# Sums of quarters on VectorE, other places for the modulation steps, and another order from the scheduler

## The chip, the cores and the metric

The kernel runs on one core of a Trainium2 chip. The metric is the time of one execution on the device, in microseconds (us), the median of several runs. One profiled execution gives the trace from which the rows below are read. All tensors are float32; no product is left at lower precision than two halves give (below).

## What is computed

Two transformer blocks in a chain, on 512 tokens `x` and 256 context tokens `ctx` of 1024 features (768 together). The first has two layers, an even one (gated linear attention and differential attention) and an odd one (a state space mixer), each followed by a gated feed-forward network; the second block is a feed-forward network, a mixer of window attention and a gated scan, and another feed-forward network. What the change touches is the feed-forward network and the modulation vectors:

```python
def swiglu(h, w_in, w_out):            # h: tokens x 1024, w_in: 1024 x 5632, w_out: 2816 x 1024
    gate, up = jnp.split(h @ w_in, 2, axis=-1)
    return (jax.nn.silu(gate) * up) @ w_out

mod_x = jax.nn.silu(c) @ mod_w[layer] + mod_b[layer]        # 6 vectors of 1024 for x,
mod_c = jax.nn.silu(c_ctx) @ mod_w[layer] + mod_b[layer]    # and 6 for the context
...
x = layer_norm(ALPHA * x + gf_x * swiglu(x * (1.0 + scf_x) + shf_x, ...), ...)
...
mod = (jax.nn.silu(c) @ w_ada[l] + b_ada[l])                # second block: 9 vectors of 1024
```

## The kernel before

Every float32 operand of a product is split into a high and a low half (`split`: ScalarE casts the high half, L64, VectorE subtracts to get the low one, L65), and each product is three matmuls. A weight (`weight`, `wcols`, `wrows`) is loaded by a DMA on SyncE's queue and split, all under a priority that lets the scheduler start it early (`WPRIO`, 400). In the trace `whi` and `wlo` are a weight's halves, `hhi` and `hlo` those of the tokens.

The work runs stage by stage: the even mixer to 470 us of the trace, its output projection and layer norm to 543, the first feed-forward network to some 1060, the odd mixer to 1700, the second network to 2098, the third to 2700, the mixer of the second block to 3250, the last network to the end. The first and the third network work on all 768 tokens, and their first product is done by quarters: tokens, weights and results are cut in two by two, and seven products of quarters, with sums before and after, take the place of eight. These two first products run from 543 to 905 and from 2098 to 2475 us.

`Quarters` keeps the tokens. `put` writes a token tile to DRAM and splits it; `sums` (L418) reads the tiles back when all are there and makes three sums `ts` of quarters (L428, L430 on VectorE, L429 on GpSimd), splits them to `tq`, and makes a fourth, `ts4` (L431, GpSimd), which `fourth` later splits in place of a quarter of the tokens. `first_product_quarters` opens with the first two of the 22 column blocks of the weight done plainly (`whole`: L524 is the silu of the gate on ScalarE, L525 the product with the second half on VectorE, both in `lg`), for the first half of the tokens and then for the second. This covers the time until the sums are there. The body then runs through the remaining 20 blocks in pairs of products (`order`). For each block, `load` fetches two weights `sr` and makes two sums on GpSimd (`sx` and one in place), and `weight` makes two more (all four by L502). `run` takes the results apart (`c`, `p`, `u`, `g`, L567 to L586).

The modulation vectors of later stages are made a step at a time in between. `mod_steps` gives ten steps for a set of one or two vectors: eight parts (a 512 KB DMA, and on VectorE L228 or L230, 128x1024, for each vector into its `acc`), `finish` (L236 adds the bias row, matmuls sum over the partitions, a DMA writes the row to DRAM) and `turn` (a DMA reads the row back as `fmrow`, L255, TensorE transposes it, L257). Steps wait in the list `c.fill`, and `run_fill(n)` puts the next n of them into the program: after each block of a product, and at other places.

The order of the instructions on each engine is set by the scheduler of the library, which takes the program in the order in which it is written, with the priorities above (modulation parts have -150), and estimates when each can start.

Of the kernel before, what the change touches and what calls it, by code (L numbers as in the profile page):

```python
# [8 lines left out]
F32 = mybir.dt.float32  # L9
# [3 lines left out]
ALU = mybir.AluOpType  # L13
# [3 lines left out]
P = 128  # L17
D = 1024
KT = D // P
WPRIO = 400  # L20
# [369 lines left out]
class Quarters:  # L390
# [27 lines left out]
    def sums(self, pool):  # L418

        c, nc = self.c, self.c.nc  # L420
        rest = []
        for i in range(self.half):
            f1, f2 = (pool.tile([P, KT, P], F32, tag=f"f{j}", name=c.nm("f"), bufs=2) for j in range(2))
            nc.sync.dma_start(f1, self.fd[i])
            nc.sync.dma_start(f2, self.fd[i + self.half])
            s = pool.tile([P, 3, 4, P], F32, tag="ts", name=c.nm("ts"), bufs=1)
            s4 = pool.tile([P, 4, P], F32, tag="ts4", name=c.nm("ts4"), bufs=self.half)
            nc.vector.tensor_tensor(s[:, 0], f2[:, :4], f1[:, :4], ALU.subtract)  # L428
            nc.gpsimd.tensor_tensor(out=s[:, 2], in0=f2[:, 4:], in1=f2[:, :4], op=ALU.subtract)  # L429
            nc.vector.tensor_tensor(s[:, 1], f2[:, 4:], s[:, 0], ALU.subtract)  # L430
# [44 lines left out]
LEAD = 2  # L475


def first_product_quarters(c, h, T, w_in, gd, nfill, pool):
# [3 lines left out]
    nc = c.nc  # L482
# [16 lines left out]
    raw = {}  # L499

    def sums(o, x, y, op):
        nc.gpsimd.tensor_tensor(out=o, in0=x, in1=y, op=op)  # L502

    def load(j):
        with c.tc.high_priority(offset=WPRIO):
            r = []
# [4 lines left out]
            r.append(pool.tile([P, 4, P], F32, tag="sx", name=c.nm("sx"), bufs=2))  # L511
            raw[j] = r
            sums(r[4], r[0], r[2], ALU.subtract)
            sums(r[2], r[2], r[3], ALU.add)

    with c.tc.tile_pool(name=c.nm("fs"), bufs=1) as fp:
        ws = [[c.wcols(w_in, o + j * P) for o in (0, FFN_H)] for j in range(LEAD)]

        def whole(j, v, outs):
# [7 lines left out]
            c.run_fill(nfill)  # L527
# [3 lines left out]
        fourth = h.sums(fp)  # L531
# [4 lines left out]
        fourth()  # L536
# [7 lines left out]
    with c.tc.tile_pool(name=c.nm("fm"), bufs=1) as mp:  # L544
        W, S, X = {}, {}, {}

        def weight(j, i, hi, lo):
# [5 lines left out]
            if i == 1:  # L553
                sums(r[0], r[3], r[4], ALU.subtract)
            elif i == 2:
                sums(r[1], r[1], r[0], ALU.subtract)
            W[j, i] = hi, lo

        def run(j, i):
# [23 lines left out]
            elif i == 3:  # L583
# [592 lines left out]
def main(c, I, out, stop=None):  # L1176
# [7 lines left out]

    def accs(pool):
        return lambda: pool.tile([P, D], F32, tag="acc", name=c.nm("acc"))
# [91 lines left out]
    with tc.tile_pool(name="mix0", bufs=1) as mp:  # L1278
        mix = mp.tile([P, 6, D], F32, name="mix")
        og, od = mix[:, :, :512], mix[:, :, 512:]  # L1280
        with tc.tile_pool(name="dif", bufs=1) as dp:
# [10 lines left out]
            with tc.tile_pool(name="gla", bufs=1) as gp:  # L1292
# [5 lines left out]
                c.fill += block1(0, 2, "gm0", "row") + block1(0, 4, "scf0", "fm") + block1(0, 3, "shf0", "fm")  # L1298
# [55 lines left out]
    with tc.tile_pool(name="modp1", bufs=2) as mq:  # L1354
        modp[0] = accs(mq)
        c.fill += block1(0, 5, "gf0", "row") + block1(1, 1, "scm1", "fm") + block1(1, 0, "shm1", "fm")
        c.fill += block1(1, 2, "gm1", "row", False) + block1(1, 4, "scf1", "fm", False)
        c.fill += block1(1, 3, "shf1", "fm", False)
# [3 lines left out]
        ffn(c, h, 768, I["ffn_w_in"][0], I["ffn_w_out"][0], ln, (1, 1))  # L1362
# [32 lines left out]
    with tc.tile_pool(name="modp2", bufs=2) as mq:  # L1395
        modp[0] = accs(mq)
        c.fill += block1(1, 5, "gf1", "row", False) + block2(0, "fm") + block2(1, "fm") + block2(2, "row")
# [19 lines left out]
    with tc.tile_pool(name="modp3", bufs=2) as mq:  # L1417
        modp[0] = accs(mq)
        c.fill += block2(3, "fm") + block2(4, "fm") + block2(5, "row", False) + block2(6, "fm", False)
        c.fill += block2(7, "fm", False) + block2(8, "row", False)  # L1420
# [3 lines left out]
        ffn(c, h, 768, I["ffn1_w_in_2"][0], I["ffn1_w_out_2"][0], ad, (1, 1))  # L1424
# [745 lines left out]
```

## Time and profile before

| | us |
|---|---|
| median of 3 runs | 3641.51 (3630.83 to 3643.37) |
| the profiled run | 3632.67 |
| its span, first to last instruction | 3630.9 |
| TensorE busy (PE) | 3412.6 |
| VectorE busy (DVE) | 2372.8 |
| ScalarE busy (ACT) | 1641.7 |
| GpSimd busy (POOL) | 649.9 |

The span is 1.8 us shorter than the profiled run, and that run is 8.8 us faster than the median. The mean granted clock of TensorE over the span is 0.974 of full speed; most of the loss lies in a few stretches.

### The profile page before, as it was taken

The page shows a single profiled execution, that of the slowest core. Times are in us where ns is not written, and L with a number is a line of the kernel's source. Part 1 is how long each engine was busy: PE and PEld are TensorE (multiplying, and loading weights), DVE is VectorE, ACT ScalarE, POOL GpSimd, SP SyncE. Part 2 cuts the span into 40 slices and gives each one's busy share as a digit, 9 for nine tenths or more (in the row PEclk, how much of TensorE's full clock was granted, in tenths as well). Part 3 has the DMA queues.
Part 4 walks back from the last instruction along what each step waited for, and adds up shares of the span by engine and source line. Part 5 has one row for each costly group of instructions (what it writes and reads, how often), then busy time and mean ns, then how long its engine had stood idle before and what let it go on. Part 6 is the DMA issues. An engine that isn't in the chain of part 4 may idle for free.

```text
span 3630.9 us, 48754 instructions
## 1 busy us (share of the span) xinstructions
PE 3412.6 (94%) x18316; PEld 2903.6 (80%) x18316; DVE 2372.8 (65%) x3578; ACT 1641.7 (45%) x2719; POOL 649.9 (18%) x481
## 2 busy tenths in 40 slices
PE   8999987999989999988999979999999999999998
PEld 5877776999778877767887769998787798878887
DVE  6766667676687577766566786766766585663235
ACT  5335533444345555533334634343556454553234
POOL 0001124433020354443000133430000000000000
PEclk9999998999999999989999989999999999999999
DMA  6330135443774333344666753436751122354356
GB/s 226 111 88 27 47 116 181 134 125 102 244 249 149 87 101 103 101 157 160 219 196 203 261 189 104 134 114 221 252 183 40 52 63 73 108 180 151 119 169 217
DMA packets 446834, 522.53 MB, mean 144 GB/s; under 512 B 21272, under 2 KB 357268, under 8 KB 446597
## 3 DMA queue, kind: packets, MB, share of 16 engines
q1 hardware_dynamic: 446597, 519.41, 45.0%
q8 instruction: 144, 2.36, 0.3%
q14 instruction: 93, 0.76, 0.1%
HBM read 452.49 MB, written 62.64 MB: 142 GB/s over the span
## 4 chain that ended last, share of the span: by engine, by line
PE 34%; issue 9%; DVE 4%; DMA 4%; ACT 2%; POOL 1%; SPq 0%; DVEq 0%; POOLq 0%; ACTq 0%
PE big L99 7%; PE big L113 5%; PE px L113 5%; PE px L496 4%; PE px L99 4%; PE big L496 3%; DMA gr<-gd 1%; DVE wlo L65 1%; PE mm L1606 1%; PE mm L1779 1%; PE big L1571 1%; ACT whi L64 1%; PE mm L1600 1%; PE big L1569 0%; DVE acc L230 0%
## 5 line engine op out<-in xcount | busy, mean ns | idle before, releaser
L65 DVE TENSOR_TENSOR wlo<-raw,whi 128x1024 fp32r<-128x1024 f32 (+1 forms) x444 | 542.3, 1226 | 476.3 <-ACT whi L64 440.9
L64 ACT CAST whi<-raw 128x1024 fp32r<-128x1024 f32 (+1 forms) x444 | 457.7, 1033 | 673.7 <-PE big L99 216.4
L99 PE MATMUL big<-hhi,whi 128*128 128x512 f32 (+1 forms) x1312 | 444.9, 364 | 10.0 <-ACT hhi L64 5.8
L99 PE MATMUL big<-hlo,whi 128*128 128x512 f32 (+1 forms) x1312 | 437.6, 359 | 5.3 <-DVE hlo L65 5.3
L99 PE MATMUL big<-hhi,wlo 128*128 128x512 f32 (+1 forms) x1312 | 439.4, 360 | 0.0
L133 POOL TENSOR_TENSOR s<-s,mhalf 128x1 f32<-128x1 f32 (+1 forms) x106 | 76.3, 721 | 1989.0 <-DVE s L131 1976.0
L99 PEld LDWEIGHTS big<-hhi,whi 128*128 128x128 f32 x1312 | 237.6, 192 | 55.1 <-issue 7.8
L99 PEld LDWEIGHTS big<-hlo,whi 128*128 128x128 f32 x1312 | 236.4, 191 | 42.9 <-DVE hlo L65 6.6
L99 PEld LDWEIGHTS big<-hhi,wlo 128*128 128x128 f32 x1312 | 236.3, 191 | 37.2 <-issue 1.9
L230 DVE SCALAR_TENSOR_TENSOR acc<-graw,silu_c,acc 128x1024 f32<-128x1024 f32 x168 | 223.9, 1355 | 33.5 <-DMA graw<-in_mod_w_dram 16.4
L65 DVE TENSOR_TENSOR wlo<-sr,whi 128x512 fp32r<-128x512 f32 x240 | 187.0, 813 | 60.6 <-ACT whi L64 59.9
L64 ACT CAST whi<-sr 128x512 fp32r<-128x512 f32 x240 | 139.3, 618 | 183.5 <-PE big L496 84.4
L113 PE MATMUL px<-whi,hhi 128*128 128x256 f32 (+1 forms) x712 | 213.2, 302 | 0.1
L113 PE MATMUL px<-wlo,hhi 128*128 128x256 f32 (+1 forms) x712 | 211.1, 299 | 0.0
L113 PE MATMUL px<-whi,hlo 128*128 128x256 f32 (+1 forms) x712 | 210.5, 299 | 0.0
L113 PE MATMUL big<-wlo,ghi 128*128 128x512 f32 x616 | 193.5, 395 | 2.4 <-DVE wlo L65 2.3
L113 PE MATMUL big<-whi,glo 128*128 128x512 f32 x616 | 192.3, 393 | 0.0
L113 PE MATMUL big<-whi,ghi 128*128 128x512 f32 x616 | 192.2, 394 | 0.0
L496 PE MATMUL px<-tq,whi 128*128 128x384 f32 x640 | 165.1, 338 | 4.8 <-DVE tq L65 2.5
L496 PE MATMUL big<-hhi,whi 128*128 128x384 f32 x416 | 143.6, 345 | 26.2 <-DVE lg L525 22.9
L64 ACT CAST ghi<-gr 128x256 fp32r<-128x256 f32 (+1 forms) x176 | 79.7, 458 | 150.0 <-DMA gr<-gd 91.6
L496 PE MATMUL big<-hhi,wlo 128*128 128x384 f32 x416 | 142.8, 344 | 1.7 <-DVE wlo L65 1.7
(594 smaller groups left out, 8265.0 us busy)
## 6 DMA issues: line engine op xcount, KB each, us to landing
raw<-in_ffn_w_out_dram SPq DMA_DIRECT2D x176, 512.0 KB
raw<-in_ffn_w_in_dram SPq DMA_DIRECT2D x96, 512.0 KB
graw<-in_mod_w_dram SPq DMA_DIRECT2D x80, 512.0 KB
sr<-in_ffn_w_in_dram SPq DMA_DIRECT2D x80, 512.0 KB
graw<-in_w_ada_dram SPq DMA_DIRECT2D x72, 512.0 KB
raw<-in_mix_w_in_dram SPq DMA_DIRECT2D x42, 512.0 KB
raw<-in_ssd_w_in_dram SPq DMA_DIRECT2D x41, 512.0 KB
gr<-gd SPq DMA_DIRECT2D x88, 192.0 KB
```

What stands on the lines that cost most here:

```text
L64: self.nc.scalar.copy(hi, src)
L65: self.nc.vector.tensor_tensor(lo, src, hi.bitcast(F32), ALU.subtract)
L99: self.nc.tensor.matmul(out, lhsT=w_[:, k, :], rhs=x_[:, k, t0 : t0 + tn], start=st, stop=sp)
L113: self.nc.tensor.matmul(out, lhsT=h_[:, t0 : t0 + P], rhs=w_[:, n0 : n0 + nn], start=st, stop=sp)
L133: nc.gpsimd.tensor_tensor(out=r, in0=v, in1=self.mhalf[:, :n], op=ALU.pow)
L230: nc.vector.scalar_tensor_tensor(a, raw, v[:, k : k + 1], a, ALU.mult, ALU.add)
L496: nc.tensor.matmul(out, lhsT=w_[:, k], rhs=b_[:, k], start=start and k == 0 and w_ is wh and b_ is bh, stop=stop and k == 3 and w_ is wl, ...
L1571: nc.tensor.matmul(sc[:, o : o + kn], lhsT=qs[b][r, tt], rhs=kl[kv][r, k0 : k0 + kn], start=False, stop=True)
L1600: nc.tensor.transpose(pt[:, i - i0 : i - i0 + P], p[:, i : i + P], c.ident)
L1606: nc.tensor.matmul(po[r, :], lhsT=v[:, u, kv * 64 : kv * 64 + 64], rhs=pT[:, i * P : (i + 1) * P], start=i == 0, stop=i == len(keys) - 1)
L1779: nc.tensor.matmul(pa[:, ts_], lhsT=QK[:, 1, ts_], rhs=Q[:, ts_], start=True, stop=True)
```

## The change

Five things are changed.

- The sums of quarters go from GpSimd to VectorE: the two of each token tile in `Quarters.sums` and the four of each block in `first_product_quarters`. The first two of a block are made where its weight is split first and no longer in `load`; `ts4` is made after the split and kept in another pool, and `fourth` runs after four pairs of the body instead of ahead of it.
- No modulation steps are put in by `whole`, nor by the first two blocks of the body. The rest takes two at each block instead of one.
- The first pairs of weights of the body have a priority of 50 in place of 400.
- `mods` sets the order of the modulation steps: the last step of a set (`turn`) comes behind the fifth step of the next.
- The scheduler orders the whole program by its timeline model.

```diff
     def sums(self, pool, keep):
...
-            s4 = pool.tile([P, 4, P], F32, tag="ts4", name=c.nm("ts4"), bufs=self.half)
+            s4 = keep.tile([P, 4, P], F32, tag="ts4", name=c.nm("ts4"), bufs=self.half)
             nc.vector.tensor_tensor(s[:, 0], f2[:, :4], f1[:, :4], ALU.subtract)
-            nc.gpsimd.tensor_tensor(out=s[:, 2], in0=f2[:, 4:], in1=f2[:, :4], op=ALU.subtract)
             nc.vector.tensor_tensor(s[:, 1], f2[:, 4:], s[:, 0], ALU.subtract)
-            nc.gpsimd.tensor_tensor(out=s4, in0=f1[:, 4:], in1=s[:, 1], op=ALU.subtract)
+            nc.vector.tensor_tensor(s[:, 2], f2[:, 4:], f2[:, :4], ALU.subtract)
             o = slice(i * P, (i + 1) * P)
             c.split(s, self.t[0][:, :, :, o], self.t[1][:, :, :, o])
+            nc.vector.tensor_tensor(s4, f1[:, 4:], s[:, 1], ALU.subtract)
...
     def sums(o, x, y, op):
-        nc.gpsimd.tensor_tensor(out=o, in0=x, in1=y, op=op)
+        nc.vector.tensor_tensor(o, x, y, op)
...
-            sums(r[4], r[0], r[2], ALU.subtract)
-            sums(r[2], r[2], r[3], ALU.add)
...
-            c.run_fill(nfill)
...
-        fourth()
...
             if i == 1:
+                sums(r[4], r[0], r[2], ALU.subtract)
+                sums(r[2], r[2], r[3], ALU.add)
                 sums(r[0], r[3], r[4], ALU.subtract)
...
-                c.run_fill(nfill)
+                if j >= LEAD + 2:
+                    c.run_fill(nfill)
...
-            with c.tc.high_priority(offset=WPRIO):
+            if s == 4:
+                fourth()
+            with c.tc.high_priority(offset=WPRIO if s > 8 else 50):
...
+    def mods(*sets):
+
+        late = None
+        for steps in sets:
+            for i, f in enumerate(steps[:-1]):
+                c.fill.append(f)
+                if i == 4 and late:
+                    c.fill.append(late)
+            late = steps[-1]
+        c.fill.append(late)
...
-        ffn(c, h, 768, I["ffn_w_in"][0], I["ffn_w_out"][0], ln, (1, 1))
+        ffn(c, h, 768, I["ffn_w_in"][0], I["ffn_w_out"][0], ln)
...
-    with _tile.TileContext(nc) as tc:
+    with _tile.TileContext(nc, schedule_with_timeline_sim=True) as tc:
```

What the scheduler makes of it is seen in the order of the instructions. First VectorE where the first product by quarters begins, from the first `lg` (gate times second half of a plain block) to the second. `acc` is a modulation vector, `ts` a sum of token quarters, `sr` a raw weight. Before:

```order
L525 TENSOR_TENSOR lg_5256<-big_5179,lg_5256 128x384
L230 SCALAR_TENSOR_TENSOR acc_5260<-graw_5426,silu_c,acc_5260 128x1024
L230 SCALAR_TENSOR_TENSOR acc_5261<-graw_5426,silu_c,acc_5261 128x1024
L230 SCALAR_TENSOR_TENSOR acc_5260<-graw_5482,silu_c,acc_5260 128x1024
L65 TENSOR_TENSOR wlo_5497<-sr_5358,whi_5496 128x512 x2
L230 SCALAR_TENSOR_TENSOR acc_5261<-graw_5482,silu_c,acc_5261 128x1024
L65 TENSOR_TENSOR wlo_5535<-sr_5365,whi_5534 128x512 x2
L65 TENSOR_TENSOR wlo_5573<-sr_5358,whi_5572 128x512
L65 TENSOR_TENSOR wlo_5573<-sr_5360,whi_5572 128x512
L525 TENSOR_TENSOR lg_5314<-big_5180,lg_5314 128x384
```

And now:

```order
L523 TENSOR_TENSOR lg_5256<-big_5179,lg_5256 128x384
L228 TENSOR_SCALAR acc_5951<-graw_5953,silu_c 128x1024
L228 TENSOR_SCALAR acc_5952<-graw_5953,silu_c 128x1024
L230 SCALAR_TENSOR_TENSOR acc_5951<-graw_5957,silu_c,acc_5951 128x1024
L230 SCALAR_TENSOR_TENSOR acc_5952<-graw_5957,silu_c,acc_5952 128x1024
L230 SCALAR_TENSOR_TENSOR acc_5951<-graw_6083,silu_c,acc_5951 128x1024
L428 TENSOR_TENSOR ts_5316<-f_5313,f_5312 128x512
L430 TENSOR_TENSOR ts_5316<-f_5313 128x512
L230 SCALAR_TENSOR_TENSOR acc_5952<-graw_6083,silu_c,acc_5952 128x1024
L523 TENSOR_TENSOR lg_5308<-big_5180,lg_5308 128x384
```

The splits of the body's first weights no longer stand ahead of the second `lg`; four steps of the modulation became six, and eleven more follow before the third `tq` (three in the order before).

Next VectorE at the start of the second product by quarters, up to the `hlo` with which the last token tile is split. `hTf` is that tile, turned; L982 and L131 are its norm. Before:

```order
L65 TENSOR_TENSOR hlo_17292<-hTf_18089,hhi_17291 128x8x128
L131 TENSOR_SCALAR s_18132<-s_18130 128x1
L230 SCALAR_TENSOR_TENSOR acc_18280<-graw_18501,silu_c,acc_18280 128x1024
L230 SCALAR_TENSOR_TENSOR acc_18279<-graw_18722,silu_c,acc_18279 128x1024
L230 SCALAR_TENSOR_TENSOR acc_18280<-graw_18722,silu_c,acc_18280 128x1024
L230 SCALAR_TENSOR_TENSOR acc_18279<-graw_18848,silu_c,acc_18279 128x1024
L282 TENSOR_SCALAR hTf_18137<-mm_18138,ada_0x,fm_m0x 128x128
L282 TENSOR_SCALAR hTf_18137<-mm_18147,ada_0x,fm_m0x 128x128
L230 SCALAR_TENSOR_TENSOR acc_18280<-graw_18848,silu_c,acc_18280 128x1024
L65 TENSOR_TENSOR hlo_17292<-hTf_18137,hhi_17291 128x8x128
```

And now, for both of the last two tiles:

```order
L236 TENSOR_TENSOR acc_18971<-acc_18971,brow_19536 1x1024
L983 TENSOR_SCALAR s_18124<-s_18118,s_18122 128x1
L1081 TENSOR_TENSOR y_15032<-y_15032,lng_17283 128x1024
L282 TENSOR_SCALAR hTf_18089<-mm_18090,ada_0x,fm_m0x 128x128
L1085 TENSOR_TENSOR y_15032<-y_15032,lnb_17285 128x1024
L282 TENSOR_SCALAR hTf_18089<-mm_18099,ada_0x,fm_m0x 128x128
L131 TENSOR_SCALAR s_18132<-s_18130 128x1
L65 TENSOR_TENSOR hlo_17292<-hTf_18089,hhi_17291 128x8x128
L282 TENSOR_SCALAR hTf_18137<-mm_18138,ada_0x,fm_m0x 128x128
L282 TENSOR_SCALAR hTf_18137<-mm_18147,ada_0x,fm_m0x 128x128
L65 TENSOR_TENSOR hlo_17292<-hTf_18137,hhi_17291 128x8x128
```

The steps between the two `hlo` are gone; all 18 of that set, its last (L236) at the top of this piece, now stand ahead of both.

Last TensorE at the end of the first attention. L918 and L919 are its scores, L950 its transposes, L959 its values; L113 are matmuls of a projection that fills its gaps. Before:

```order
L918 MATMUL big_4203<-dks_3737,dqs_3735 128x512
L919 MATMUL big_4203<-dks_3738,dqs_3735 128x512
L959 MATMUL mm_4181<-ddv,mix 128x128 x2
L918 MATMUL big_4203<-dks_3737,dqs_3735 128x256
L919 MATMUL big_4203<-dks_3738,dqs_3735 128x256
L113 MATMUL px_3916<-wlo_3803,hhi_379 128x256
L113 MATMUL px_3916<-whi_3802,hlo_380 128x256
L113 MATMUL px_3916<-whi_3808,hhi_379 128x256
```

And now, 70 rows earlier, with no projection left:

```order
L951 MATMUL mm_3583<-cfs,dp_3526 128x128 x4
L919 MATMUL big_3760<-dks_3317,dqs_3315 128x512
L920 MATMUL big_3760<-dks_3318,dqs_3315 128x512
L919 MATMUL big_3760<-dks_3317,dqs_3315 128x256
L920 MATMUL big_3760<-dks_3318,dqs_3315 128x256
L951 MATMUL mm_3589<-cfs,dp_3526 128x128 x2
L960 MATMUL mm_3593<-ddv,mix 128x128 x2
L951 MATMUL mm_3774<-cfs,dp_3566 128x128 x4
```

The last matmul of the projection stood 26 rows ahead of the attention's end and now stands 107 rows ahead of it.

## Rows read from the trace of the kernel before

**Rows 1.** The page, part 1: busy us, share of the span, instructions of each engine.

```profile
PE 3412.6 (94%) x18316; PEld 2903.6 (80%) x18316; DVE 2372.8 (65%) x3578; ACT 1641.7 (45%) x2719; POOL 649.9 (18%) x481
```

**Rows 2.** Stretches: length, busy PE, PEld, DVE, ACT, POOL, granted clock, DMA share, GB/s.

```profile
440.00:460.00 20.00, 15.42 (x83) 12.13 (x82) 12.14 (x33) 12.91 (x34) 2.57 (x4) 0.83 0.18 54
580.00:630.00 50.00, 30.40 (x124) 28.33 (x123) 38.30 (x37) 16.99 (x28) 25.87 (x17) 0.73 0.52 174
630.00:905.00 275.00, 266.80 (x1514) 261.72 (x1513) 195.77 (x258) 118.08 (x227) 108.01 (x69) 0.99 0.38 120
2110.00:2180.00 70.00, 44.68 (x216) 42.69 (x215) 57.74 (x62) 29.33 (x52) 24.85 (x16) 0.76 0.53 172
2180.00:2475.00 295.00, 284.74 (x1607) 279.25 (x1606) 196.75 (x258) 123.86 (x237) 107.41 (x72) 0.99 0.35 111
2700.00:3100.00 400.00, 396.42 (x2513) 334.08 (x2512) 262.46 (x598) 214.78 (x382) 6.45 (x5) 1.00 0.22 64
```

**Rows 3.** TensorE in time, 580 to 630: start, duration, instruction, [idle before <- releaser].

```profile
591.67 0.69 PE L496 MATMUL big<-hhi,whi 128*128 128x384 f32 x1 [5.52 <-DVE lg L525]
...
610.92 0.69 PE L496 MATMUL big<-hhi,whi 128*128 128x384 f32 x1 [5.80 <-DVE lg L525]
...
620.95 0.69 PE L496 MATMUL px<-tq,whi 128*128 128x384 f32 x1 [2.51 <-DVE tq L65]
```

**Rows 4.** The same of TensorE, 2110 to 2180.

```profile
2118.78 1.97 PE L275 MATMUL mm<-cfs,xr 128*128 128x128 f32 x8 [5.21 <-ACT xr L1172]
...
2134.50 1.01 PE L496 MATMUL px<-hhi,whi 128*128 128x384 f32 x2 [2.96 <-ACT hhi L64]
...
2170.44 0.69 PE L496 MATMUL big<-hhi,whi 128*128 128x384 f32 x1 [11.53 <-DVE lg L525]
```

**Rows 5.** ScalarE in time at both starts.

```profile
587.62 1.14 ACT L64 CAST whi<-sr 128x512 fp32r<-128x512 f32 x2 [6.54 <-POOL sr L502]
...
2154.56 1.14 ACT L64 CAST whi<-sr 128x512 fp32r<-128x512 f32 x2 [6.95 <-POOL sr L502]
```

**Rows 6.** VectorE in time at both starts.

```profile
575.21 3.67 DVE L230 SCALAR_TENSOR_TENSOR acc<-graw,silu_c,acc 128x1024 f32<-128x1024 f32 x3
...
610.32 0.55 DVE L525 TENSOR_TENSOR lg<-big,lg 128x384 f32<-128x384 f32 x1
...
619.15 1.75 DVE L65 TENSOR_TENSOR tq<-ts,tq 128x1536 fp32r<-128x1536 f32 x1
...
2143.50 0.68 DVE L428 TENSOR_TENSOR ts<-f,f 128x512 f32<-128x512 f32 x1
...
2158.08 1.76 DVE L428 TENSOR_TENSOR ts<-f,f 128x512 f32<-128x512 f32 x1
...
2175.16 2.49 DVE L65 TENSOR_TENSOR wlo<-sr,whi 128x512 fp32r<-128x512 f32 x4
```

**Rows 7.** Groups of instructions: count, busy us, mean ns, idle before and releaser.

```profile
L502 POOL TENSOR_TENSOR sr<-sr 128x512 f32<-128x512 f32 x80 | 121.6, 1520 | 88.1 <-DVE wlo L65 84.0
L431 POOL TENSOR_TENSOR ts<-f,ts 128x512 f32<-128x512 f32 x6 | 10.5, 1757 | 6.7 <-DVE ts L430 6.7
...
L230 DVE SCALAR_TENSOR_TENSOR acc<-graw,silu_c,acc 128x1024 f32<-128x1024 f32 x168 | 223.9, 1355 | 33.5 <-DMA graw<-in_mod_w_dram 16.4 <-DMA graw<-in_w_ada_dram 16.3
L65 DVE TENSOR_TENSOR wlo<-sr,whi 128x512 fp32r<-128x512 f32 x240 | 187.0, 813 | 60.6 <-ACT whi L64 59.9 <-PE px L496 0.3
```

**Rows 8.** TensorE's waits for a turned row (us, times, longest), and one row's DMAs.

```profile
PE mm L257 <- DMA fmrow<-row_m4c: 4.0, 1, 4.0
PE mm L257 <- DMA fmrow<-row_m6x: 2.6, 1, 2.6
PE mm L257 <- DMA fmrow<-row_m7x: 2.0, 1, 2.0
...
L248 SPq DMA_DIRECT2D row_m0c<-acc x1: 235/235/235, 1854.7 to 1854.7; - x1
L255 SPq DMA_DIRECT2D fmrow<-row_m0c x1: 264/264/264, 1860.8 to 1860.8; - x1
```

More of the change, by code (lines that the diff above doesn't have):

```diff
@@ L416, in factors, with sums @@
                 {(0, 0): q(0), (1, 0): q(1), (0, 1): q(2), (1, 1): q(3)})
-    def sums(self, pool):
+    def sums(self, pool, keep):
         c, nc = self.c, self.c.nc
@@ L501, in sums @@
     def sums(o, x, y, op):
-        nc.gpsimd.tensor_tensor(out=o, in0=x, in1=y, op=op)
+        nc.vector.tensor_tensor(o, x, y, op)
     def load(j):
+        r = []
         with c.tc.high_priority(offset=WPRIO):
-            r = []
             for b, o in enumerate((0, FFN_H)):
@@ L510, in load @@
                 r += [x[:, :4], x[:, 4:]]
-            r.append(pool.tile([P, 4, P], F32, tag="sx", name=c.nm("sx"), bufs=2))
-            raw[j] = r
-            sums(r[4], r[0], r[2], ALU.subtract)
-            sums(r[2], r[2], r[3], ALU.add)
+        r.append(pool.tile([P, 4, P], F32, tag="sx", name=c.nm("sx"), bufs=2))
+        raw[j] = r
     with c.tc.tile_pool(name=c.nm("fs"), bufs=1) as fp:
@@ L526, in whole @@
             nc.sync.dma_start(gd[j][:, v * n : v * n + n], g)
-            c.run_fill(nfill)
         for j in range(LEAD):
             whole(j, 0, (one(j), two(j)))
-        fourth = h.sums(fp)
+        fourth = h.sums(fp, pool)
         for j in range(LEAD, LEAD + 2):
@@ L1297, in main @@
                 modp[0] = lambda: df.pair()[:, :D]
-                c.fill += block1(0, 2, "gm0", "row") + block1(0, 4, "scf0", "fm") + block1(0, 3, "shf0", "fm")
+                mods(block1(0, 2, "gm0", "row"), block1(0, 4, "scf0", "fm"), block1(0, 3, "shf0", "fm"))
                 c.run_fill(3)
@@ L1355, in main @@
         modp[0] = accs(mq)
-        c.fill += block1(0, 5, "gf0", "row") + block1(1, 1, "scm1", "fm") + block1(1, 0, "shm1", "fm")
-        c.fill += block1(1, 2, "gm1", "row", False) + block1(1, 4, "scf1", "fm", False)
-        c.fill += block1(1, 3, "shf1", "fm", False)
+        mods(block1(0, 5, "gf0", "row"), block1(1, 1, "scm1", "fm"), block1(1, 0, "shm1", "fm"),
+             block1(1, 2, "gm1", "row", False), block1(1, 4, "scf1", "fm", False), block1(1, 3, "shf1", "fm", False))
         ln = LnTail(c, None, I, 0, 1, 6, {v: f"gf0{v}" for v in "xc"}, xdt(0),
@@ L1396, in main @@
         modp[0] = accs(mq)
-        c.fill += block1(1, 5, "gf1", "row", False) + block2(0, "fm") + block2(1, "fm") + block2(2, "row")
+        mods(block1(1, 5, "gf1", "row", False), block2(0, "fm"), block2(1, "fm"), block2(2, "row"))
         ln = LnTail(c, None, I, 1, 1, 4, {"x": "gf1x"}, xdt(2), lambda: ada_sc(0, 0, "xc"), xd[3], "x", 768,
@@ L1418, in main @@
         modp[0] = accs(mq)
-        c.fill += block2(3, "fm") + block2(4, "fm") + block2(5, "row", False) + block2(6, "fm", False)
-        c.fill += block2(7, "fm", False) + block2(8, "row", False)
+        mods(block2(3, "fm"), block2(4, "fm"), block2(5, "row", False), block2(6, "fm", False),
+             block2(7, "fm", False), block2(8, "row", False))
         ad = AdaTail(c, None, 6, lambda pool: ada_gate(pool, 0, 2, 0.5, "xc"),
@@ L1423, in main @@
                      out if stop == "f1" else None)
-        ffn(c, h, 768, I["ffn1_w_in_2"][0], I["ffn1_w_out_2"][0], ad, (1, 1))
+        ffn(c, h, 768, I["ffn1_w_in_2"][0], I["ffn1_w_out_2"][0], ad)
         h = ad.h
```

## The prediction, made before the changed kernel was run

> **What bounds the kernel now.** I read first the page's table of busy times, then the stretches, then the waits of TensorE in the stretches where it is not full. TensorE is busy for 94% of the span, VectorE for 65%, GpSimd for 18% [rows 1]. So a moved instruction is worth only what it does to TensorE's gaps or to its granted clock. The stretches [rows 2] show where these are. In 630 to 905 and 2180 to 2475, the bodies of the two products by quarters, TensorE is full but for 8.2 of 275 and 10.3 of 295 us, at a clock of 0.99. Where these stages begin it is not: 580 to 630 has 30.4 us of work in 50 at a clock of 0.73, 2110 to 2180 has 44.7 in 70 at 0.76. Counted as idle time plus time lost to the low clock, that is 19.6 + 0.27 x 50 = 33 us at the first start and 25.3 + 0.24 x 70 = 42 us at the second. **75 us is thus all that a perfect start of both stages could give.** The same stretches show 23% idle at the end of the first attention (440 to 460), and 99% busy in window attention (2700 to 3100), where nothing is to be won.
>
> The waits name the links. At the first start TensorE waits 5.52 and 5.80 us for `lg` on VectorE and 2.51 us for the third `tq` [rows 3]; at the second 5.21 us for `xr`, 2.96 us for `hhi` and 11.53 us for `lg` [rows 4]. ScalarE had itself waited 6.54 and 6.95 us for GpSimd's sums just before, with `lg` queued behind [rows 5]. That is the link the change cuts.
>
> **The change part by part.**
>
> *Sums to VectorE.* 172 instructions of 128x512 (4 for each of 20 weights in each stage, and 2 for each of 6 token tiles) go from GpSimd, 1.52 to 1.76 us each [rows 7], to VectorE. Alone, VectorE needs 0.68 us for one and 2.49 us for four in a row, 0.62 each; while GpSimd works the same line takes 1.76 us [rows 6]. So VectorE takes on 172 x 0.62 = 107 us, and gets contention back: the `wlo<-sr` group means 813 ns where 620 to 680 is the clean price, 240 x 0.15 = 36 to 46 us, and the `L230` group 1355 ns against 1220 to 1280, 168 x 0.1 = 17 us [rows 7]. Net about +50 us of VectorE over the 720 us of the two stages, which it has: 195.8 busy of 275 and 196.8 of 295 [rows 2]. On TensorE's path the gain is bounded by the steady gaps, 18.5 us less the 4.0 of [rows 8] and about 5 us of clock: -20. The loss is bounded by the modulation steps that the order packs into the same stretches: on VectorE they stand 9 to 12 rows later than before at the start of the body and 13 to 20 rows earlier in 820 to 1060 and 2375 to 2600, 13 to 20 x 1.22 us of work in one place: up to +15 where weights' splits wait behind it. I take **-3** (-20 to +15), since TensorE's waits there are few and short.
>
> GpSimd slows VectorE on these rows by 1.1 us each time they meet, close to GpSimd's own duration. The Trainium skill, "SBUF — State Buffer", section Terms, says that the two engines share a port pair which one instruction holds for its full length, while the other is fully blocked. The single rows agree (1.76 beside 0.68 us). By that rule each of the 172 moved instructions could have cost VectorE its whole 1.5 us, 258 us, and the move would relieve VectorE by some 150 us. The group means, which hold all meetings, show 53 to 63 us lost, and I go by them; the rule's outcome is the third rival.
>
> *First stage's start.* The diff says that no modulation step is put in here. The order shows that the scheduler draws them back: between the first `lg` and the third `tq`, VectorE now has 17 steps of the modulation (7 before), 35 instructions of 128x512, three `tq` and six of 384 columns. From [rows 6], 17 x 1.22 + 35 x 0.62 + 3 x 1.75 + 6 x 0.55 = 51 us. The first `lg` ended at 575.2, where the three steps of [rows 6] begin, so the third `tq` comes at 626; it ended at 620.9. On the way the second `lg` comes at about 583, 8 us earlier, and the first wait of 5.52 us goes; what is late next is the fourth `lg` (612 by the same count, 610.9 before) and that `tq`. So the gain is given back within 40 us: +5, less perhaps 3 us of clock as the gaps are shorter. I take **+2**, from -10 (the steps find room in waits for ScalarE) to +12.
>
> *Second stage's start.* Between the gate product of the last token tile and the first `hlo`, VectorE now has 18 modulation steps; before, 7 to the first and 12 to the second `hlo`. At 1.22 us that is 6 to 11 steps, 7 to 13 us, less about 3 us that VectorE idled there: TensorE's restart at 2134.5 moves to about 2144. From there the sums on VectorE help: 27 of 128x512, three `tq`, four of 384 columns make 24 us to the third `tq`, at 2170, about where it was. TensorE has 24 us of work from its restart to the point where it waited 11.53 us, so it gets there at 2169 and finds `lg`; before, it went on at 2170.4. So -1.5, with the clock: 0.24 x 70 = 17 us are lost there now, some of it moves from the second half to the first. I take **-3** (-12 to +10).
>
> *`run_fill` and the due times.* Fewer steps at the starts means that they go elsewhere, and the last step of a set (`turn`, L257) now stands behind five steps of the next. Its waits of 4.0, 2.6 and 2.0 us [rows 8] have then at least five steps of room, and go: -8.6. At four other sets nothing follows, or the scheduler draws `turn` up: of `m0c`, `m3c`, `scf0c` and `shf0x` only 0.3 to 6.3 us of TensorE's work now lie between the row's matmuls and the transpose. From the row's store to the issue of the reading DMA 6.1 us pass [rows 8], though nobody waited then. Each of the four can wait 0 to 6 us; I take 3, 12 in all. Net **+3** (-9 to +12).
>
> *The order by the timeline model.* Elsewhere TensorE's order differs by 1 to 3 us, except in the attentions. In the first, the projection matmuls that fill gaps are used up earlier: 107 rows of pure attention now end it where 26 did. By the rows' durations that is about 50 us unmixed in place of 18. An unmixed stretch runs 23% idle and at a clock of 0.83 [rows 2], so 32 more us of it cost at most 7 us idle and 5 us of clock, less what the earlier fill saves in its place: **+6** (0 to +12). Window attention is 99% busy and ends with some 14 unmixed pieces: **+4** (0 to +10, since there is nothing to gain). The start of the kernel: 0, within 3 either way.
>
> Sum: -3 + 2 - 3 + 3 + 6 + 4 = **+9 us**.
>
> **The rivals.**
>
> *The starts are cleared (faster).* Modulation steps stand in VectorE's order but cost nothing, because ScalarE or a DMA is what it waits for between them. For it: VectorE idles in 11.7 of 50 and 12.3 of 70 us there now. Then the 22.8 us of the three waits for `lg` go, the clock (30 us) is back, and 10 us of the small ones: -60 at best, with +13 from the attentions left: 3585 to 3610, **3595** as its middle. Against: both counts above leave VectorE no idle time. Chance 0.26.
>
> *VectorE becomes the bound in the bodies (slower).* Place: 740 to 905 and 2290 to 2475. 80 sums of 0.62 us each stage lift VectorE's busy time from 71% and 67% to some 80%, and the 13 to 20 steps drawn up (16 to 24 us) fill it for about 140 and 100 us. It decides once the backlog is larger than the distance between a weight's split and its first matmul; then each stage loses its backlog, 15 to 24 us, and some clock: +35 in all on top of +9 without the -3: **3677**. Against: low-clock stretches in the bodies are single ones today, and weights are split ahead. Chance 0.27.
>
> *Blocked by the port (a rule's outcome).* If every meeting with GpSimd cost VectorE GpSimd's whole duration, relief is 150 us and the bodies lose all their gaps: -20 in place of -3, and 3625. Chance 0.08.
>
> **How the numbers follow.** The profiled run took 3632.7 us (span 3630.9); its median sibling took 3641.5, so two of the three runs lie 9 to 11 us above the profile. +9 on the profile is 3642, on the median 3650. I predict **3645**, chance 0.39 for 3615 to 3675, the sum of the terms' ends taken as independent. The range reaches from the faster rival's good half to the slower one's: 3588 to 3685. A change within 0.5%, 18 us, is about what a measurement of this kernel can tell from none. Below 3623: 0.27 (the first rival, a little of the forecast); above 3660: 0.31 (the second rival and the forecast's upper end); between: 0.42.
>
> **What would show it.** In the profile after: in 580 to 630 no wait for the second `lg`, but waits for the third and fourth `lg` or the third `tq` on VectorE, with VectorE nearly full; at the second start a longer wait for `xr` or `hhi` and none of 11.5 us; `wlo<-sr` at 620 to 680 ns; waits at L257 on `m0c`, `m3c`, `scf0c`, `shf0x` and none on `m4c`; an unmixed end of attention of about 50 us. It is wrong if both starts run at a clock over 0.9 (first rival), or if 740 to 905 shows waits on `wlo` or `c` of over 15 us with VectorE over 90% (second rival). The largest unknown is whether modulation steps on VectorE really stand in the way of `lg`.

## The result, and the profile after

The changed kernel takes 3730.19 us (median of 4 runs, 3728.57 to 3735.56), before 3636.17 us in the runs beside it: a ratio of 1.0261, 95% interval 1.0234 to 1.0289. It is 94 us slower; the forecast was 3645 and the range ended at 3685. The profiled run's span grew from 3630.9 to 3727.6 us, by 96.7.

The page of the kernel after, part 1, and two of its groups, which answer to [rows 1] and [rows 7]:

```profile
PE 3437.5 (92%) x18316; PEld 2938.6 (79%) x18316; DVE 2415.8 (65%) x3750; ACT 1629.4 (44%) x2713; POOL 393.5 (11%) x309
...
L230 DVE SCALAR_TENSOR_TENSOR acc<-graw,silu_c,acc 128x1024 f32<-128x1024 f32 x168 | 212.2, 1279 | 54.6 <-DMA graw<-in_w_ada_dram 28.1
...
L65 DVE TENSOR_TENSOR wlo<-sr,whi 128x512 fp32r<-128x512 f32 x240 | 158.2, 683 | 27.8 <-ACT whi L64 21.2
```

The contention is gone, as forecast: `wlo<-sr` fell from 813 to 683 ns, `L230` from 1355 to 1279. That is not where 97 us can come from. Stretches of the kernel after, which answer to [rows 2] (the same places, shifted as far as the kernel runs late there):

```profile
622.00:672.00 50.00, 31.65 (x133) 29.04 (x132) 44.44 (x59) 16.92 (x30) 0.00 (x0) 0.76 0.48 158
672.00:940.00 268.00, 266.31 (x1525) 261.71 (x1524) 217.78 (x343) 120.89 (x232) 0.00 (x0) 1.00 0.44 138
2154.00:2224.00 70.00, 43.38 (x224) 41.28 (x224) 57.24 (x80) 30.21 (x50) 4.03 (x4) 0.78 0.52 167
2224.00:2510.00 286.00, 286.00 (x1632) 281.05 (x1632) 220.69 (x347) 128.07 (x243) 0.00 (x0) 1.00 0.44 137
2717.00:2951.00 234.00, 223.53 (x1333) 180.00 (x1332) 133.97 (x319) 120.93 (x240) 6.94 (x5) 0.99 0.22 65
2951.00:3001.00 50.00, 46.85 (x316) 42.21 (x315) 19.25 (x46) 22.80 (x42) 0.00 (x0) 0.97 0.11 33
3001.00:3079.00 78.00, 57.40 (x422) 55.87 (x421) 62.12 (x133) 46.71 (x55) 0.00 (x0) 0.86 0.10 29
```

Both starts are as bad as they were (31.7 of 50 and 43.4 of 70 us of work; before 30.4 and 44.7). The two bodies got better: full, at a clock of 1.00. The new hole is the last row, in the first of the two gated scans, 57.4 of 78 us at a clock of 0.86.

To see where the time went, each kernel's trace (one profiled run of each) was cut at the first or last instruction of certain lines on TensorE (the first `L336`, the last value matmul of the first attention, the first and last `L496` of each product by quarters, and so on). Durations in us; the columns to the right of "after" belong to the experiments below.

| stage | before | after | order only | code only | sums only | steps only |
|---|---|---|---|---|---|---|
| to the first projection | 43.7 | 59.1 | 58.7 | 43.2 | 45.3 | 41.9 |
| even mixer | 416.7 | 435.4 | 434.8 | 416.1 | 416.6 | 417.1 |
| its output projection and norm | 83.0 | 91.3 | 91.1 | 83.0 | 83.0 | 83.7 |
| first product by quarters | 380.4 | 372.6 | 378.4 | 357.3 | 361.8 | 392.6 |
| second product, odd mixer | 784.0 | 776.0 | 781.8 | 786.2 | 786.8 | 777.0 |
| second network, first product | 258.2 | 277.8 | 262.6 | 272.9 | 260.2 | 270.0 |
| its second product | 132.5 | 129.7 | 132.9 | 131.6 | 132.7 | 132.3 |
| first product by quarters of the third network | 382.1 | 372.7 | 381.6 | 356.5 | 355.1 | 384.8 |
| its second product | 211.8 | 202.4 | 216.5 | 205.0 | 209.9 | 205.4 |
| window attention and both scans | 453.8 | 512.4 | 510.0 | 453.2 | 455.6 | 456.8 |
| the rest | 484.7 | 498.2 | 497.3 | 487.2 | 484.8 | 484.3 |

The networks by quarters, for which the code was rewritten, gained 7.8, 9.4 and 9.4 us. Lost were 58.6 us in window attention and the scans, 18.7 in the even mixer, 15.4 ahead of it, 8.3 behind it, 13.5 in the rest, and 19.6 in the second network's first product. Apart from the last and the even mixer, where `mods` reorders the steps of three modulation vectors, none of these has a changed line; they have another order. Of the 19.6 us, 13 lie ahead of the product: its cut is the last matmul of the odd mixer's output, and from there to its own first matmul 13.4 us pass after the change and 0.2 before.

### The profile page after: what moved, and what is told of

Same layout as the page of the kernel before. It is cut to its first block, busy times and chain, and to the rows that moved or that the text cites. A ratio compares the mean times of both kernels' runs of the same rounds, so it can differ in the third digit from the quotient of the medians.

```text
span 3727.6 us, 48551 instructions
## 1 busy us (share of the span) xinstructions
PE 3437.5 (92%) x18316; PEld 2938.6 (79%) x18316; DVE 2415.8 (65%) x3750; ACT 1629.4 (44%) x2713; POOL 393.5 (11%) x309
## 4 chain that ended last, share of the span: by engine, by line
PE 68%; DVE 12%; DMA 10%; ACT 5%; issue 4%; POOL 1%; SPq 0%; DVEq 0%; ACTq 0%; POOLq 0%
PE big L99 16%; PE big L113 11%; PE px L496 9%; PE px L113 8%; PE big L496 7%; PE px L99 6%; DVE wlo L65 2%; DMA graw<-in_mod_w_dram 2%; DMA raw<-in_ffn_w_out_dram 2%; DVE acc L230 1%; DMA graw<-in_w_ada_dram 1%; ACT whi L64 1%; PE mm L1617 1%; DVE sxT L1976 1%; DMA gr<-gd 1%
## 5 line engine op out<-in xcount | busy, mean ns | idle before, releaser
L65 DVE TENSOR_TENSOR wlo<-raw,whi 128x1024 fp32r<-128x1024 f32 (+1 forms) x444 | 552.3, 1246 | 449.8 <-ACT whi L64 443.5
L230 DVE SCALAR_TENSOR_TENSOR acc<-graw,silu_c,acc 128x1024 f32<-128x1024 f32 x168 | 212.2, 1279 | 54.6 <-DMA graw<-in_w_ada_dram 28.1
L113 PE MATMUL px<-whi,hhi 128*128 128x256 f32 (+1 forms) x712 | 217.5, 308 | 18.6 <-ACT hlf L1692 15.3
L113 PE MATMUL px<-wlo,hhi 128*128 128x256 f32 (+1 forms) x712 | 214.9, 303 | 0.0
L113 PE MATMUL px<-whi,hlo 128*128 128x256 f32 (+1 forms) x712 | 212.9, 301 | 0.0
L113 PE MATMUL big<-wlo,ghi 128*128 128x512 f32 x616 | 194.3, 397 | 7.1 <-DVE wlo L65 7.0
L113 PE MATMUL big<-whi,glo 128*128 128x512 f32 x616 | 191.9, 393 | 0.0
L113 PE MATMUL big<-whi,ghi 128*128 128x512 f32 x616 | 190.1, 394 | 0.5 <-ACT whi L64 0.5
L65 DVE TENSOR_TENSOR wlo<-sr,whi 128x512 fp32r<-128x512 f32 x240 | 158.2, 683 | 27.8 <-ACT whi L64 21.2
L496 PE MATMUL px<-tq,whi 128*128 128x384 f32 x640 | 165.5, 337 | 7.0 <-DVE tq L65 4.5
L113 PEld LDWEIGHTS px<-whi,hhi 128*128 128x128 f32 x712 | 139.1, 196 | 27.8 <-ACT hlf L1692 16.5
L496 PE MATMUL big<-hhi,whi 128*128 128x384 f32 x416 | 141.1, 340 | 6.4 <-DVE lg L523 4.7
```

Source lines behind the costliest of these rows:

```text
L65: self.nc.vector.tensor_tensor(lo, src, hi.bitcast(F32), ALU.subtract)
L113: self.nc.tensor.matmul(out, lhsT=h_[:, t0 : t0 + P], rhs=w_[:, n0 : n0 + nn], start=st, stop=sp)
L230: nc.vector.scalar_tensor_tensor(a, raw, v[:, k : k + 1], a, ALU.mult, ALU.add)
L496: nc.tensor.matmul(out, lhsT=w_[:, k], rhs=b_[:, k], start=start and k == 0 and w_ is wh and b_ is bh, stop=stop and k == 3 and w_ is wl, ...
```

## Experiments: the order and the code apart

The first four kernels take the change to pieces. Order only:

```diff
-    with _tile.TileContext(nc) as tc:
+    with _tile.TileContext(nc, schedule_with_timeline_sim=True) as tc:
```

> The source of before, but ordered by the scheduler's timeline model. Theory A (the order costs, the edits help): the order alone brings the whole loss and a little more, +90 to +130 us (3730 to 3770), with the loss where the fillers of the attentions and scans are used up early: some 15 us at the start, 15 to 20 in the first attention, 25 in window attention, 40 in the gated scan, 20 in the second network's first product. Theory B (the edits cost, above all the sums on VectorE): -10 to +20 us.

Measured: 3750.83 us, ratio 1.0296 (1.0256 to 1.0335), about 105 us slower. Theory A holds; the places are those of the table, only the second network's first product is hardly among them (4 of the 20 expected).

Code only is the changed source without that line's change.

> The source of after, but ordered by the default of the scheduler. Theory A: 20 to 45 us faster than before (3590 to 3615), since the four stretches of the two networks by quarters took some 32 us less in the changed kernel's trace than in that of before. Theory B: 50 to 100 us slower than before.

Measured: 3594.17 us, ratio 0.9857 (0.9825 to 0.989), about 52 us faster, a little over what theory A asked. Theory B falls. Its starts and bodies, in stretches:

```profile
580.00:630.00 50.00, 41.44 (x221) 39.55 (x220) 46.08 (x69) 23.55 (x41) 0.00 (x0) 0.93 0.62 198
630.00:905.00 275.00, 272.91 (x1551) 265.99 (x1550) 229.76 (x352) 122.72 (x231) 0.00 (x0) 1.00 0.48 149
2110.00:2180.00 70.00, 59.45 (x309) 57.84 (x310) 63.80 (x90) 36.66 (x64) 2.71 (x3) 0.86 0.60 185
2180.00:2475.00 295.00, 294.70 (x1649) 284.61 (x1649) 225.82 (x344) 130.60 (x242) 0.00 (x0) 1.00 0.49 157
```

In the default order the starts clear in large part: 41.4 and 59.5 us of work where 30.4 and 44.7 were, clock 0.93 and 0.86 (the second stage begins 8 us earlier in this kernel; in the stretch shifted by that it is 55.9 us at 0.85). So **the order costs 115 us on the code of before and 135 us on the new code**, by the spans of the profiled runs (105 by the medians of the first); on the new code it also undoes 15 and 16 us of the gain of the two first products.

Sums only moves the 172 sums and nothing else.

```diff
-            nc.gpsimd.tensor_tensor(out=s[:, 2], in0=f2[:, 4:], in1=f2[:, :4], op=ALU.subtract)
+            nc.vector.tensor_tensor(s[:, 2], f2[:, 4:], f2[:, :4], ALU.subtract)
...
-            nc.gpsimd.tensor_tensor(out=s4, in0=f1[:, 4:], in1=s[:, 1], op=ALU.subtract)
+            nc.vector.tensor_tensor(s4, f1[:, 4:], s[:, 1], ALU.subtract)
...
-        nc.gpsimd.tensor_tensor(out=o, in0=x, in1=y, op=op)
+        nc.vector.tensor_tensor(o, x, y, op)
```

> Before with the 172 sums of quarters on VectorE and nothing else changed. Theory A with the sums as the source of the gain: 10 to 30 us faster, GpSimd's waits at both starts gone, wlo<-sr near 650 ns. Theory A with the modulation steps as its source: within 8 us of before. Theory B: 20 us or more slower.

Measured: 3602.85 us, ratio 0.9887 (0.985 to 0.9924), some 41 us faster and more than any theory had. The page of this kernel, part 1, and its bodies:

```profile
PE 3403.3 (95%) x18316; PEld 2895.7 (81%) x18316; DVE 2390.2 (67%) x3750; ACT 1643.9 (46%) x2719; POOL 385.2 (11%) x309
```

```profile
630.00:905.00 275.00, 272.87 (x1562) 268.50 (x1561) 209.49 (x333) 121.57 (x231) 0.00 (x0) 1.00 0.40 124
2180.00:2475.00 295.00, 293.34 (x1631) 282.24 (x1630) 214.15 (x330) 126.76 (x236) 0.00 (x0) 1.00 0.45 142
```

TensorE's idle time in the bodies falls from 8.2 and 10.3 us to 2.1 and 1.7, and VectorE as a whole is busy only 17 us more than before, though by the prediction's 0.62 us each 107 us of work were moved to it. This edit alone clears most of the starts: in the stretches shifted as far as the stages begin later or earlier here, the first has 37.6 us of work in 50 at a clock of 0.86, the second 56.8 in 70 at 0.88, and the wait of 11.5 us for `lg` is gone though 13 modulation steps stand between the first `lg` and the third `tq` there (14 before).

Steps only takes the new places of the modulation steps (no `run_fill` at the starts, two at each later block, `mods`) with the sums still on GpSimd:

```diff
-            c.run_fill(nfill)
...
-                c.run_fill(nfill)
+                if j >= LEAD + 2:
+                    c.run_fill(nfill)
...
-        c.fill += block2(3, "fm") + block2(4, "fm") + block2(5, "row", False) + block2(6, "fm", False)
-        c.fill += block2(7, "fm", False) + block2(8, "row", False)
+        mods(block2(3, "fm"), block2(4, "fm"), block2(5, "row", False), block2(6, "fm", False),
+             block2(7, "fm", False), block2(8, "row", False))
```

> Before with the modulation steps moved alone: none where a product by quarters begins, two at each later block, the last step of a set behind the fifth of the next; sums still on GpSimd, default order. Theory A with the sums as the source: 5 to 15 us faster, mostly the waits for a turned row (8.6 us) and a part of the starts. With the steps as the source: 20 us or more faster. Theory B: within 10 us of before.

Measured: 3658.29 us, ratio 1.0041 (1.0023 to 1.0059), 12 us slower, which no theory had (B allowed 10). By the table the steps gain 6 to 7 us behind each product by quarters (behind the third network's, 4.6 us of the waits for turned rows go; behind the first's no such wait was over 0.4 us), and lose 12 us in the first network's first product and 12 in the second network's.

The parts do not add up: -41 and +12 make -29, the code together is -52. The 23 us between, little more than the noise of the three, belong to parts that were not run alone (the priority of the first weights, the later `fourth`) or to what the parts do together; no kernel here tells which.

## Experiments: the second network, and a faster version

The second network's first product takes 12 to 15 us longer wherever the new order of the steps is, whatever the scheduler. This kernel is the changed source in the default order with the old order there:

```diff
-        mods(block1(1, 5, "gf1", "row", False), block2(0, "fm"), block2(1, "fm"), block2(2, "row"))
+        c.fill += block1(1, 5, "gf1", "row", False) + block2(0, "fm") + block2(1, "fm") + block2(2, "row")
```

> The changed source in the default order, but with the old order of the modulation steps in the second network, where its first product took 272.9 us against 258.2 before and 260.2 with the sums alone. Theory: the new order of the steps there costs it 12 to 15 us (their loads queue ahead of weights), so this kernel takes 3575 to 3590 us, 60 to 70 us less than before, and that first product 258 to 262. Rival: the longer product comes from something else (an accident of the order), and the time stays at 3590 to 3600.

Measured: 3573.53 us, ratio 0.9841 (0.9807 to 0.9874), 62 us faster than before; that first product takes 259.7 us. So the order of the steps is the cause of its 12 to 15 us. That their loads queue ahead of weights is only read (in the code-only kernel SyncE held back step loads 38.9 us for `wlo` there, here 24.3); it was not tested apart. By its median it is the fastest version of this study; its interval and the code-only kernel's overlap.

## Experiments: what the order does

Two places stayed to be explained: why the new order undoes 15 us in each first product, and what costs 59 us in window attention and the scans. The gated scan is a chain: on VectorE and ScalarE states are built, then for each head eight levels of `hQK` follow each other, each with a few matmuls (`L1790` after, `L1779` before). TensorE is kept busy meanwhile by projections: the 16 gates (`gst`) and the second heads' `hlf` and `hv`. Modulation steps and gates were thinned out together in two kernels, one in each order. They leave out seven of the eight parts of each vector that is made in the first and the third network, and the 16 gate projections, whose rows are a constant; each was run once.

```diff
+    def cut(steps):
+        return steps[:1] + [lambda: None] * 7 + steps[8:]
...
-                (pg,) = c.proj_a(W, GA + n * P, h, XSEG)
                 s = pool.tile([P, 512], F32, tag="gst", name=c.nm("gst"), bufs=1)
-                nc.scalar.copy(s, pg)
+                nc.vector.memset(s, 0.5)
```

> The changed kernel (timeline order) with two things left out: seven of the eight parts of each modulation vector that is made during the two networks by quarters, and the 16 gate projections that fill the gated scan (their rows are a constant). Read by stage against the next kernel, which is the same in the default order. Theory M1 (the order draws steps and fillers up, so that steps stand in the way at the starts and the scan is left bare): without steps the two first products by quarters take the same in both orders within 5 us each (15 us apart with them: 372.6 and 372.7 against 357.3 and 356.5), and without the gate projections window attention plus both scans are at most 25 us apart (59 us with them: 512.4 against 453.2). Theory M2 (the timeline order's interleaving of the engines is itself worse on the chip, whatever there is to fill): 10 to 15 us apart in each first product and 45 us or more in the attention and scans.

> The same with the same two things left out, in the scheduler's default order. M1: window attention plus both scans lose clearly less than the 88 us of TensorE that the 16 projections took (16 x 24 x 0.23), since the scan shows its own chain then: 395 to 425 us in place of 453. M2: they lose all of it, 365 to 375 us. The first products by quarters: 345 to 357 us each in both theories.

Measured, by the same cuts of the traces:

| us | timeline order | default order | apart | apart in the full code |
|---|---|---|---|---|
| first product by quarters | 353.0 | 351.5 | 1.5 | 15.3 |
| the third network's | 357.7 | 351.6 | 6.1 | 16.2 |
| window attention and scans | 440.3 | 394.9 | 45.4 | 59.2 |

In the products M1 holds in the main (the 6.1 is over its 5 us): without most of the modulation steps the order costs 1.5 and 6.1 us in place of 15 and 16, so **the steps that the order draws back to the starts are what undoes the gain there**, all but a few us. In the scan M1 fails by its own measure and M2's mark is met: with nothing of the gates left to draw up, 45 us remain. That the default order has 395 us, 58 less for an estimated 88 us of matmuls less, shows that the scan has a chain of its own of which some 30 us then come to light.

So the second heads' projections were held back next, by a true dependency. Their weights are multiplied by ones made from the first scan's output:

```diff
                     if hp:
+                        hg.hold = hgs.tile([P, 256], F32, name="hold")
+                        nc.vector.tensor_scalar(hg.hold, o[3][:, :256], 0.0, 1.0, ALU.mult, ALU.add)
                         hg.forget(1, 0)
...
-            hi, lo = self.weight(src, half, n)
+            hi, lo = self.weight(src, half, n, scale)
```

> The changed kernel (timeline order) with one true dependency added: the weights of the second heads' projections (forget and values) of the gated scan are multiplied by ones that are made from the first scan's output, so the scheduler can't draw these projections into the first scan. Between the end of window attention and the end of the first scan the changed kernel takes 128 us, before 88, and the version with less to fill, in timeline order, still 125 against 92. Theory M3 (projections drawn up stand ahead of the scan's own links on all engines): 85 to 105 us there, the second scan's part 150 to 175, and the whole 20 to 45 us faster than the changed kernel (3685 to 3710). Theory M2 (the interleaving within the scan itself is worse): 118 us or more there, and the whole at 3730 or above.

Measured: 3737.53 us, ratio to before 1.0261 (1.0231 to 1.0291): no gain on the changed kernel. But the first scan's part, from the end of window attention, takes 86.3 us, in M3's range, and the second 193 us, over it (150 in the changed kernel). So M3 is right about the first scan and wrong about the whole, where M2's 3730 or above came. Stretches of this kernel, the first scan's part and what follows:

```profile
2962.00:3048.00 86.00, 58.02 (x324) 51.28 (x323) 59.71 (x148) 35.79 (x61) 0.00 (x0) 0.84 0.02 7
3048.00:3175.00 127.00, 121.20 (x802) 111.01 (x802) 54.39 (x86) 49.22 (x74) 5.33 (x6) 0.99 0.29 87
3175.00:3241.00 66.00, 62.98 (x438) 57.39 (x436) 52.05 (x116) 41.92 (x52) 0.00 (x0) 1.00 0.20 64
```

Shown is that the drawn-up projections stood in the first scan's way (128 us with them, 86 without). But the first scan is now bare, 58 of 86 us at a clock of 0.84, and the projections run by themselves for 55 us (3056.6 to 3111.3), in a stretch where VectorE has 54 of 127 us to do. Nothing is left over to go beside the chain. In the kernel before the first scan had it:

```profile
2926.00:2988.00 62.00, 62.00 (x424) 55.96 (x423) 56.11 (x122) 37.19 (x46) 0.00 (x0) 1.00 0.20 61
```

62 us, TensorE full, VectorE 56 of 62, at full clock. In that kernel the results of four of the first seven gates are copied in this stretch (2929 to 2966 us); in the changed kernel five were ready inside window attention (2853 to 2897), two while the states are built (2966.0 and 2974.5), and none between the levels. The last pair holds the gates too, until window attention has ended, with and without the first hold:

```diff
+                late.append(hgs.tile([P, 256], F32, name="late"))
+                nc.vector.tensor_scalar(late[0], oT[0].bitcast(F32)[:, 3, 256:], 0.0, 1.0, ALU.mult, ALU.add)
...
-                (pg,) = c.proj_a(W, GA + n * P, h, XSEG)
+                (pg,) = c.proj_a(W, GA + n * P, h, XSEG, scale=late[0][:, :P])
```

> The kernel with the second heads' projections held (e8) and, by the same means, the gate projections held until the end of window attention, still in timeline order. From the end of the stage before to the end of the second scan the default order takes 453 us, the changed kernel 512 and the kernel with one hold 512. Theory P (it matters only that the fillers are left for the scans): window attention back at 205 to 212 us, and 455 to 475 in all. Theory Q (the order also spends them at once where they come free, beside the states and the keys, so the chain of the eight levels stays bare): window attention at 205 to 212, but 485 to 505 in all.

> The changed kernel with the gate projections held until the end of window attention and the second heads' projections free. P: 455 to 475 us from the end of the stage before to the end of the second scan. Q: the projections stand in the first scan's way as in the changed kernel, and gates and projections together make its part 140 us or more; 490 to 515 in all.

Measured in one run each: 3737.65 and 3716.31 us, where the run of before beside them took 3640.95. From the end of the stage before to the end of the second scan 511.4 and 489.7 us. Window attention alone fell from 234 to 193 us in both, under the 205 to 212 expected. The stretches with both held: window attention, the states of the first scan, its eight levels, the rest.

```profile
2728.00:2922.00 194.00, 183.88 (x1172) 150.22 (x1170) 120.22 (x308) 107.79 (x226) 6.94 (x5) 0.98 0.15 42
2922.00:2983.00 61.00, 60.68 (x323) 51.95 (x323) 25.07 (x51) 24.18 (x46) 3.13 (x7) 1.00 0.33 100
2983.00:3043.00 60.00, 35.87 (x172) 32.76 (x170) 45.33 (x109) 22.38 (x29) 0.00 (x0) 0.70 0.03 9
3043.00:3240.00 197.00, 188.55 (x1238) 171.99 (x1236) 107.44 (x203) 91.08 (x126) 13.61 (x19) 0.95 0.26 78
```

Theory P fails. Q has the mechanism; its ranges miss a little (511 over 505, 489.7 just under 490). Of the seven gates that belong to the first scan, six stand, in this kernel's order on TensorE, ahead of the first of the levels, in the 61 us while the states are built and VectorE does 25 us of work, and the seventh's matmuls between the first three groups of `hQK`; when VectorE's long chain begins, TensorE has 36 of 60 us to do, at a clock of 0.70. **In these kernels the timeline order spends a filler as soon as it can start; to set when fillers come free is not enough, they have to be kept for the chain**, as they are in the default order (by the program's order and the priorities, which was not tested). With the gates held and the projections not, 23 of the 59 us come back.

What stays open: the 15 us ahead of the first projection and the 19 us of the even mixer. There the traces only show the same sign: TensorE waits 5.5 us for rows of a later stage's vectors that the new order turns ahead of the first projection, and in the even mixer idles 31 us where it idled 21 and loses 40 us to the low clock where it lost 17 (granted 0.91 and 0.96). No kernel was made to test these.

## Why the prediction was wrong

*What bounds the kernel* held: TensorE's gaps and its clock decided every experiment.

*Sums to VectorE* had the right mechanism and the wrong size. The term was -3 out of -20 to +15; measured alone it is -41. In the bodies the far end came true, 14.7 us of gaps gone and the clock at 1.00. The working counted contention in two groups only, 53 to 63 us. In the sums-only kernel the instructions that VectorE had before are shorter by some 86 us, summed by their durations, and only 42 of them lie in these two groups (`wlo<-sr` 813 to 684 ns, `L230` 1355 to 1291); 19 are in `g<-c,c` (1026 to 552 ns), 10 in `wlo<-sx` (940 to 684), most of the rest in the tokens' sums. The prediction's 258 us, worked out from the rule of the Trainium skill, "SBUF — State Buffer", Terms, are three times these 86, but they pointed the right way against the two groups. Some 24 of the 46 us gained in the two products by quarters came in their first 300 matmuls, at the starts that the next two terms took up.

*The two starts* were read rightly from the order. TensorE in time in the kernel after, first start, which answers to [rows 3]:

```profile
632.89 0.69 PE L496 MATMUL px<-hhi,whi 128*128 128x384 f32 x1 [4.72 <-ACT lg L522]
...
639.92 0.44 PE L496 MATMUL px<-hhi,whi 128*128 128x384 f32 x1 [2.82 <-DVE lg L523]
...
647.45 0.69 PE L496 MATMUL big<-hhi,whi 128*128 128x384 f32 x1 [3.74 <-DVE lg L523]
...
660.17 0.69 PE L496 MATMUL px<-tq,whi 128*128 128x384 f32 x1 [4.50 <-DVE tq L65]
```

and second start, which answers to [rows 4]:

```profile
2179.03 1.97 PE L275 MATMUL mm<-cfs,xr 128*128 128x128 f32 x8 [17.59 <-ACT xr L1173]
...
2186.15 1.97 PE L275 MATMUL mm<-cfs,xr 128*128 128x128 f32 x8 [5.15 <-ACT xr L1173]
...
2191.08 1.01 PE L496 MATMUL px<-hhi,whi 128*128 128x384 f32 x2 [2.96 <-ACT hhi L64]
```

The first has waits for the later `lg` and the third `tq`, the second a long wait for `xr` and none of 11.5 us for `lg`, as forecast: the steps stand in the way, and what the sums gain is given back. The thinned kernels show it. To the 300th of a product's 1872 matmuls it takes 90.1 and 87.7 us before, 86.1 and 88.9 after (-4 and +1, where the terms were +2 and -3), and 73.4 and 75.9 in the code-only kernel.

*Turned rows*: the three waits of [rows 8] are gone, and of the four new ones, 3 us each in the sum (12 in all), one came, with 2.2:

```profile
PE mm L257 <- DMA fmrow<-row_scf0c: 2.2, 1, 2.2
```

*The order by the timeline model* is the step that failed. It stood with +6 and +4, and 0 for the start; measured alone it is about 105 us. For window attention the working said that a stretch that is 99% busy has nothing to win, took +4 with an end of +10, and went on. It did not ask what keeps it at 99%: a scan that is a chain on VectorE, covered by fillers that the default order keeps for it. The new order was priced by the 14 unmixed pieces at the end of window attention alone; the scan behind it was not in the sum. Of the 58.6 us measured, 27 lie in window attention (207 to 234), which takes in gates that ran later before, and 40 in the first scan, which then lacks them (88 to 128); the second scan gains 8. TensorE's waits from the end of window attention to the end of the second scan, in the kernel after:

```profile
PE mm L1790 <- DVE hQK L1785: 16.4, 5, 4.7
PE px L113 <- ACT hlf L1692: 10.3, 4, 5.2
PE mm L1790 <- ACT hQK L1781: 2.8, 1, 2.8
```

The kernel before has no wait there worth a row. The same goes for the even mixer: its unmixed end was priced (+6 for 50 us; it became 69 us, 425.4 to 494.5, at a clock of 0.80), the clock all along it was not, and the mixer lost 18.7.

*The second network* was left out, since its code seemed unchanged. But `mods` changes the order of its steps too: +19.6, of which 12 to 15 come with that edit.

*The rivals*: the faster one's middle, 3595, is what the code without the order takes (3594), by luck: its sum has 13 us of loss in the attentions, which that kernel has not, and its reason was steps that stand in the order and cost nothing, while at the first start of that kernel only 4 stand between the first `lg` and the third `tq` (16 in the changed kernel). The slower one had the right sign by the wrong mechanism: VectorE never bounded the bodies, where TensorE was full (and its terms add up to 3680, not 3677). The range was too narrow since the order, which alone reaches every stage, had 25 us of it at its upper ends (12, 10 and 3).

## What to carry to other kernels

A switch that re-orders the whole program has to be priced in every stage and first in the fullest one: an engine at 99% beside a chain can be full because something was kept for that moment, as here, and then it has the most to lose. Read for each chain what goes beside it before and after, and count the fillers that are spent earlier. A bundle of edits that act in different places should be timed one by one: here one part was worth -41 us, one +12 and one +105, and they did not add up to the whole.

## What the runs showed of the hardware

The 172 instructions that left GpSimd take 682 to 691 ns each on VectorE, and VectorE was busy only 17 us longer: with these gone from GpSimd (sums-only kernel), its other instructions became some 86 us shorter. In the two products by quarters, groups that read two tiles of SBUF gained (`g<-c,c` fell from 1026 to 552 ns); the 120 in the same places that read one operand from PSUM, where TensorE leaves its results (`c<-big,u`, `c<-big,p`), took 550 to 554 ns before and 548 to 552 in the sums-only kernel. And idle time in small pieces cost twice here: in the first scan of the kernel after 21 us of 78 were idle, and 11 more were lost to the half clock (granted 0.86), while the same chain in the kernel before, fully covered, had 1.00.
